# A hybrid encoder on one core: the block products' operand sums moved to the fifth and sixth tile of each feed-forward layer, and five pairs of tiles in block form instead of six

## The chip, the cores and the metric

The kernel runs on one core of one Trainium2 chip. The metric is device time in microseconds (us). Engines: TensorE (PE) multiplies, VectorE (DVE) and ScalarE (ACT) do the elementwise work, SyncE (SP) issues most DMAs.

## The reference

Two layers work on a sequence of 1040 columns (16 learned ones and 1024 inputs) of width 1024. Each layer adds a mixer and then a feed-forward part. The change lies in the feed-forward part alone:

```python
def swiglu(h, w_gate_up, w_down):
    gate, up = jnp.split(h @ w_gate_up.astype(h.dtype), 2, axis=-1)
    return (jax.nn.silu(gate) * up) @ w_down.astype(h.dtype)
```

`w_gate_up` is 1024 x 5632, so gate and up have 2816 rows each: 22 tiles of 128.

## The kernel before

All activations lie transposed, 128 features of a tile by the columns. A float32 product is made of three matmuls: each operand is split in a high part (ACT, a copy) and a low part (DVE, the rest), and high x high, high x low and low x high are added in PSUM. Weights are split as they arrive: `w_op` (line 1104 the high part on ACT, line 1105 the low part on DVE). `prod` (lines 1122, 1125, 1126) makes one product of four k-blocks, 12 matmuls.

The gate and up products run over tiles `f` = 0 to 21 (the first to the twenty-second), and a tile's two products are made in a form with seven products in place of eight (P1 to P7), the sums of weights S1 to S4 (lines 1464, 1465, 1473 or 1485, 1486) and sums of activations T1 to T4. The columns are two halves of 520 in the first layer and of 512 in the second (`l` = 1, where the first 16 columns are not needed). The first layer makes each product in two parts of 260 columns (`NJ` = 2), the second in one of 512. Products are evicted from PSUM by ACT (lines 1505, 1578) and DVE (1509, 1518 or 1566, 1569, 1573, 1582). `row_end` multiplies gate and up with the scale, applies silu, multiplies (lines 1438 to 1441) and stores the row to DRAM (1445); 1447 makes a difference for the later product.

**Block form.** The product P3 (S4 of the weights with B22 of the activations) of two neighbouring tiles is made together: the two S4 and the four quarters of B22 are taken as 2 x 2 blocks, and seven products of quarter size (6 matmuls each, 260 or 256 columns; `block`, lines 1530 to 1532) stand in place of eight. The even tile of a pair keeps its S4 in a tile `keep` (line 1485). The odd tile makes its own (line 1473) and four sums of the two (lines 1476 to 1479, tile `sm`), which are split by `w_op`. The activations' side needs sums of the quarters of B22, made once per layer: `block_operands` (lines 1422 to 1426 the sums in a scratch tile `t`, 1430 and 1431 their splits). Pairs are the tiles with `6 <= f < 18`, the seventh to the eighteenth.

**What sets the order.** Each engine works through its instructions in one fixed order. A scheduler makes it at build time from program order, priorities, dependences and buffers. A tile of a tag with `n` buffers waits until the tile before it in that buffer is read out. The tag "c" has two buffers, which `t`, `keep`, `sm` and the fourth tile's row (`early[3]`) share. Weights use two buffers of the tag "raw" and five of "ck2" (names raw and rw). `after(x, y)` makes `x` wait for `y`. `block_operands` is called behind the fifth tile (half of the sums: `TB[0]`, `TB[1]`) and behind the sixth (the other half, which needs a result of the first, `less`).

Of the kernel before, what the change touches and what calls it, by code (L numbers as in the profile page):

```python
# [11 lines left out]
ALU = mybir.AluOpType  # L12
# [30 lines left out]
def trunk(ctx: ExitStack, tc: tile.TileContext, xT, w_in, w_ba, w_out, w_gu, w_dn,  # L43
# [15 lines left out]
    def row(tag, dt=F32, bufs=1):  # L59
        return sb.tile([128, L], dt, tag=tag, bufs=bufs, name=nm(tag))  # L60
# [4 lines left out]
    def c4k(tag="c"):  # L65
        return sb.tile([128, L], F32, tag="c", bufs=2, name=nm(tag))
# [18 lines left out]
    def after(ins, prev):  # L85

        if prev is not None:
            tc.add_manual_dep(ins.ins, prev.ins.name, dep, reason="order")
        return ins
# [6 lines left out]
    tt = nc.vector.tensor_tensor  # L96
# [133 lines left out]
    def new_x(tags):  # L230
        (t0, t1, t2), r = tags
        A, B, C = big(t0, F32R), big(t1, F32R), big(t2, F32R)
        R = [row(r, F32R, 3) for _ in range(3)] + [row(r + "f", F32R)]
        return [(A[:, k, :], B[:, k, :]) for k in range(4)] + [(C[:, k, :], R[k]) for k in range(4)]


    x = new_x(S[0])
# [76 lines left out]
    for l in range(DEPTH):  # L314
# [24 lines left out]
        def trow():  # L339
            return row(Y[1], F32, 3)  # L340
# [360 lines left out]
        for pos, i in enumerate(seq):  # L701
# [4 lines left out]
            late = pos < (2, 1)[l]  # L706
            if pos < len(opened):
                t = opened[pos]
            else:
                t = trow()  # L710
# [72 lines left out]
        for i in range(4):  # L783
            t = trow()
# [3 lines left out]
            v = trow() if i % 2 == 0 else row(Y[1] + "f")  # L788
# [209 lines left out]
        for i in range(4):  # L998
            t = trow() if i < 2 else hb[1][:, i, :] if i < 3 else y3
# [28 lines left out]
        E = (L - o0) // 4  # L1028
# [105 lines left out]
        def part(t, z, j):  # L1134

            v = half(t[:, o0:L], z)
            return v[:, j, :] if NJ == 2 else v
# [10 lines left out]
        NE = 4  # L1148
# [33 lines left out]
        for m in range(KT + 2):  # L1182
# [11 lines left out]
            k = m - 2  # L1194
# [161 lines left out]
        def t_pair(t):  # L1356
            p, i = SEVEN[t // NP], t % NP
            hi, lo = t_slot(t)
            r = dw.pop(("b", t), None)
            held.pop(t, None)  # L1360
            if p in ("P5", "P6"):
                r = t_raw(i)
            elif p == "P7":
                behind(tt(out=r, in0=t_raw(i), in1=r, op=ALU.subtract))
            elif p == "P4":
                b21, r = r, t_raw(i)
                behind(tt(out=r, in0=b21, in1=r, op=ALU.subtract))
            act(out=hi, in_=r, func=AF.Copy)  # L1368
            behind(tt(out=lo, in0=r, in1=hi.bitcast(F32), op=ALU.subtract))
            if p == "P3":  # L1370
                tt(out=t_raw(i), in0=r, in1=t_raw(i), op=ALU.subtract)
# [14 lines left out]
        def down_begins(p):  # L1386
# [11 lines left out]
            elif p is p1_[2]:  # L1398
# [2 lines left out]
                w_unit(4)  # L1401
                t_load(3)
                t_pair(3)
        TB, us, rows, less = [], [], [], [None]

        def halves(t, n):
            return t[:, 0:n], t[:, n:2 * n]

        def quarter(k, j):
            return [t[:, k:k + 2, E * j:E * j + E] for t in T["B22"]]  # L1410

        def block_rows():
            rows.extend(row(Y[1], F32R, 3) for _ in range(3))
            rows.append(row(X[1], F32R, 3))
            us.extend(row(X[1], F32, 3) for _ in range(2))

        def block_operands(i):

            (b11, c11), (b12, c12), (b21, c21), (b22, c22) = ([t.bitcast(F32) for t in quarter(k, j)] for k in (0, 2) for j in (0, 1))
            x, cx, y, cy, p, q = (b22, c22, b12, c12, b21, c21) if i else (b12, c12, b11, c11, b22, c22)  # L1420
            va, vb = (t.rearrange("p (k e) -> p k e", k=2) for t in halves(c4k("t"), 2 * E))
            after(tt(out=va, in0=x, in1=y, op=ALU.subtract), row_before)
            tt(out=vb, in0=cx, in1=cy, op=ALU.subtract)
            tt(out=va, in0=va, in1=vb, op=ALU.add)
            tt(out=vb, in0=p, in1=less[0] if i else va, op=ALU.subtract)
            tt(out=vb, in0=vb, in1=q, op=ALU.add)
            less[0] = vb
            for r, v in zip(rows[i:i + 2], (va, vb)):
                h, w = (t.rearrange("p (k e) -> p k e", k=2) for t in halves(r, 2 * E))
                act(out=h, in_=v, func=AF.Copy)  # L1430
                tt(out=w, in0=v, in1=h.bitcast(F32), op=ALU.subtract)
                TB.append((h, w))

        def row_end(f, g, u, adds):

# [14 lines left out]
        row_before = None  # L1450
        first_of = None
        for f in range(FT):
            paired = 6 <= f < 18
            even, odd = paired and f % 2 == 0, paired and f % 2 == 1
            A11, A12, A21, A22 = raw4("raw"), raw4("raw"), raw4("ck2"), raw4("ck2")
            dma(A11, w_gu[l, f, 0, :, 0:4, :])
# [150 lines left out]
                row_end(f, g, u, adds)  # L1607
            if f == NE - 1:
                block_rows()
            if f in (NE, NE + 1):  # L1610
                block_operands(2 * (f - NE))


        hb = [big(X[0][0]), big(X[0][1])]
# [42 lines left out]
        for u, (p, b, m) in enumerate(UNITS):  # L1657
            if b == 1 and p in FIRST:
                dh, z = FIRST[p]
                q = 4 * dh + m  # L1660
# [13 lines left out]
            for j in range(NJ):  # L1674
# [10 lines left out]
                if b == NBK - 1:  # L1685
                    dh, z, op = TO[p]
                    h = part(hr[4 * dh + m], z, j)
                    read_out[u] = tt(out=h, in0=pin(ps), in1=h, op=op)

        if not last:  # L1690
            x = new_x(Y)
# [6 lines left out]
        else:  # L1698
# [22 lines left out]
            for (n0, n1) in FIN:  # L1721
                e = (n1 - n0) // 4
# [7 lines left out]
                for m in range(KT):  # L1730
                    h = hr[m][:, n0:n1]
# [93 lines left out]
```

## Time and profile before

| | us |
|---|---|
| timed runs, median of 3 | 2468.67 (2467.69 to 2473.94) |
| the profiled execution | 2466.03 |
| its span, first to last instruction | 2464.3 |
| PE busy in it | 2438.2 |
| DVE busy | 1834.9 |
| ACT busy | 1081.9 |

Times in the profile's rows are counted from the start of the span. A row of the timeline gives the start, the duration, the engine, the line, the output and inputs by name, the shape, and in brackets how long the engine had been idle and what ended that. In the table by stretches each engine has its busy time and its number of instructions, then come the granted clock of PE as a share (PEclk), the DMA engines' busy share and GB/s. A row of the waits reads: who waited for whom, us in total, times, longest. The gate and up products of the first layer run from 567.92 to 1020.77 us (first and last start), those of the second up to 2234.84.

### The profile page before, as it was taken

The page shows a single profiled execution, that of the slowest core. Times are in us where ns is not written, and L with a number is a line of the kernel's source. Part 1 is how long each engine was busy: PE and PEld are TensorE (multiplying, and loading weights), DVE is VectorE, ACT ScalarE, POOL GpSimd, SP SyncE. Part 2 cuts the span into 40 slices and gives each one's busy share as a digit, 9 for nine tenths or more (in the row PEclk, how much of TensorE's full clock was granted, in tenths as well). Part 3 has the DMA queues.
Part 4 walks back from the last instruction along what each step waited for, and adds up shares of the span by engine and source line. Part 5 has one row for each costly group of instructions (what it writes and reads, how often), then busy time and mean ns, then how long its engine had stood idle before and what let it go on. Part 6 is the DMA issues. An engine that isn't in the chain of part 4 may idle for free. (4 is left out here: it accounts for less than half of the span.)

```text
span 2464.3 us, 45203 instructions
## 1 busy us (share of the span) xinstructions
PE 2438.2 (99%) x17602; PEld 2256.7 (92%) x17602; DVE 1834.9 (74%) x3436; ACT 1081.9 (44%) x2028; POOL 66.3 (3%) x157
## 2 busy tenths in 40 slices
PE   9999999999999999999999999999999999999998
PEld 8999999999999999999999988998978788888887
DVE  6888346769888887977657984457797888778775
ACT  6654434536333333444445543345453333334544
POOL 0120000000000000000001100000000000000002
PEclk9999999999999999999999999999999999999999
DMA  4445345534222224674224453445332222337641
GB/s 134 160 156 185 118 134 158 182 101 134 100 78 104 84 86 137 223 243 143 92 81 155 155 179 111 152 144 194 121 124 98 82 94 99 119 130 251 198 136 69
DMA packets 201322, 335.27 MB, mean 136 GB/s; under 512 B 23404, under 2 KB 88356, under 8 KB 201108
## 3 DMA queue, kind: packets, MB, share of 16 engines
q1 hardware_dynamic: 172996, 293.83, 36.0%
q10 hardware_dynamic: 25936, 34.19, 4.3%
q0 software_dynamic: 2176, 4.36, 0.6%
q8 instruction: 138, 2.26, 0.4%
q14 instruction: 76, 0.62, 0.1%
HBM read 250.31 MB, written 81.99 MB: 135 GB/s over the span
## 5 line engine op out<-in xcount | busy, mean ns | idle before, releaser
L168 PE MATMUL pacc<-a,whi 128*128 128x346 f32 (+1 forms) x800 | 260.1, 326 | 0.7 <-ACT whi L138 0.4
L170 PE MATMUL pacc<-a,wlo 128*128 128x346 f32 (+1 forms) x800 | 259.0, 325 | 0.1
L168 PE MATMUL pacc<-b,whi 128*128 128x346 f32 (+2 forms) x672 | 232.4, 347 | 0.0
L170 PE MATMUL pacc<-b,wlo 128*128 128x346 f32 (+2 forms) x672 | 231.5, 346 | 0.0
L169 PE MATMUL pacc<-a,whi 128*128 128x346 f32 (+1 forms) x681 | 221.8, 326 | 0.2 <-DVE a L189 0.2
L138 ACT ACTIVATE whi<-raw 128x512 fp32r<-128x512 f32 x166 | 104.4, 631 | 236.8 <-PE pacc L169 195.1
L169 PE MATMUL pacc<-b,whi 128*128 128x346 f32 (+2 forms) x580 | 200.1, 345 | 0.0
L139 DVE TENSOR_TENSOR wlo<-raw,whi 128x512 fp32r<-128x512 f32 x166 | 114.0, 688 | 53.5 <-ACT whi L138 52.8
L168 PEld LDWEIGHTS pacc<-a,whi 128*128 128x128 f32 x800 | 150.5, 188 | 3.0 <-issue 1.0
L170 PEld LDWEIGHTS pacc<-a,wlo 128*128 128x128 f32 x800 | 150.7, 189 | 1.4 <-issue 0.8
L170 PEld LDWEIGHTS pacc<-b,wlo 128*128 128x128 f32 x672 | 126.4, 188 | 10.2 <-issue 1.7
L168 PEld LDWEIGHTS pacc<-b,whi 128*128 128x128 f32 x672 | 126.4, 188 | 9.8 <-issue 0.8
L169 PEld LDWEIGHTS pacc<-a,whi 128*128 128x128 f32 x681 | 128.3, 188 | 4.1 <-issue 2.1
L169 PEld LDWEIGHTS pacc<-b,whi 128*128 128x128 f32 x580 | 109.2, 188 | 7.9 <-issue 1.0
L1104 ACT ACTIVATE whi<-rw 128x512 fp32r<-128x512 f32 (+1 forms) x82 | 49.8, 615 | 107.4 <-PE pacc L1125 36.1
L1104 ACT ACTIVATE b<-rw 128x512 fp32r<-128x512 f32 (+1 forms) x63 | 38.7, 620 | 102.3 <-PE pacc L1125 29.0
L331 DVE TENSOR_TENSOR b<-pacc,rstd 128x346 f32<-128x346 f32 (+1 forms) x63 | 32.3, 513 | 49.0 <-PE pacc L170 46.3
L1104 ACT ACTIVATE a<-rw 128x512 fp32r<-128x512 f32 (+1 forms) x63 | 38.5, 618 | 64.4 <-PE pacc L1125 17.2
L331 DVE TENSOR_TENSOR a<-pacc,rstd 128x346 f32<-128x346 f32 (+2 forms) x59 | 32.6, 553 | 42.5 <-PE pacc L170 41.9
L1105 DVE TENSOR_TENSOR wlo<-rw,whi 128x512 fp32r<-128x512 f32 (+1 forms) x82 | 54.1, 666 | 9.9 <-ACT whi L1104 9.4
L1368 ACT ACTIVATE P<-a 128x512 fp32r<-128x512 f32 x63 | 38.3, 625 | 25.4 <-PE pb L1684 19.7
L1368 ACT ACTIVATE P<-b 128x520 fp32r<-128x520 f32 x63 | 37.2, 628 | 27.1 <-PE pacc L1684 20.1
(1129 smaller groups left out, 8019.0 us busy)
## 6 DMA issues: line engine op xcount, KB each, us to landing
raw<-in_w_in SPq DMA_DIRECT2D x110, 256.0 KB
raw<-in_w_gu SPq DMA_DIRECT2D x104, 256.0 KB
rw<-in_w_gu SPq DMA_DIRECT2D x88, 256.0 KB
rw<-in_w_dn SPq DMA_DIRECT2D x90, 192.0 KB
rec<-vkd SPq DMA_DIRECT2D x61, 256.0 KB
raw<-in_w_out SPq DMA_DIRECT2D x48, 256.0 KB
b<-ad SPq DMA_DIRECT2D x45, 260.0 KB
a<-ad SPq DMA_DIRECT2D x45, 256.0 KB
```

The costliest lines, as they stand in the source:

```text
L138: whi_done[0] = hasten(wpr, lambda: act(out=hi, in_=raw[:, 0:kk, :], func=AF.Copy))
L139: whi_done[1] = hasten(wpr, lambda: tt(out=lo, in0=raw[:, 0:kk, :], in1=hi.bitcast(F32), op=ALU.subtract))
L168: mm(ps[:, :n], wh, xh[:, n0:n1], start=(i == 0), stop=False)
L169: mm(ps[:, :n], wh, xl[:, n0:n1], start=False, stop=False)
L170: last_mm[0] = mm(ps[:, :n], wl, xh[:, n0:n1], start=False, stop=(i == K - 1))
L331: tt(out=t[:, n0:n1], in0=ps, in1=rstd[:, n0:n1], op=ALU.mult)
L1104: hasten(wpr, lambda: act(out=hi, in_=src, func=AF.Copy))
L1105: hasten(wpr, lambda: tt(out=lo, in0=src, in1=hi.bitcast(F32), op=ALU.subtract))
L1368: act(out=hi, in_=r, func=AF.Copy)
```

## The change

The tiles in block form are now those with `8 <= f < 18`, so the seventh and eighth tile get P3 of their own. `block_operands` is called twice behind the sixth tile: the first call makes the operands 0, 1 and 3 (7 sums), the second operand 2 (3 sums). The second sum of each call waits for the fifth tile's row (`gate`); the first (`cx` less `cy`) waits for nothing but its buffer. The number of sums (10) and splits (4) per layer stays.

```diff
-        TB, us, rows, less = [], [], [], [None]
+        TB, us, rows, gate = {}, [], [], []
...
-        def block_operands(i):
+        def block_operands(late):
 
             (b11, c11), (b12, c12), (b21, c21), (b22, c22) = ([t.bitcast(F32) for t in quarter(k, j)] for k in (0, 2) for j in (0, 1))
-            x, cx, y, cy, p, q = (b22, c22, b12, c12, b21, c21) if i else (b12, c12, b11, c11, b22, c22)
             va, vb = (t.rearrange("p (k e) -> p k e", k=2) for t in halves(c4k("t"), 2 * E))
-            after(tt(out=va, in0=x, in1=y, op=ALU.subtract), row_before)
-            tt(out=vb, in0=cx, in1=cy, op=ALU.subtract)
-            tt(out=va, in0=va, in1=vb, op=ALU.add)
-            tt(out=vb, in0=p, in1=less[0] if i else va, op=ALU.subtract)
-            tt(out=vb, in0=vb, in1=q, op=ALU.add)
-            less[0] = vb
-            for r, v in zip(rows[i:i + 2], (va, vb)):
-                h, w = (t.rearrange("p (k e) -> p k e", k=2) for t in halves(r, 2 * E))
+            x, cx, y, cy = (b22, c22, b12, c12) if late else (b12, c12, b11, c11)
+
+            def put(n, v):
+                h, w = (t.rearrange("p (k e) -> p k e", k=2) for t in halves(rows[n], 2 * E))
                 act(out=h, in_=v, func=AF.Copy)
                 tt(out=w, in0=v, in1=h.bitcast(F32), op=ALU.subtract)
-                TB.append((h, w))
+                TB[n] = h, w
+
+            tt(out=vb, in0=cx, in1=cy, op=ALU.subtract)
+            after(tt(out=va, in0=x, in1=y, op=ALU.subtract), gate[0])
+            tt(out=va, in0=va, in1=vb, op=ALU.add)
+            put(2 if late else 0, va)
+            for n, p, q, less in () if late else ((1, b22, c22, va), (3, b21, c21, vb)):
+                tt(out=vb, in0=p, in1=less, op=ALU.subtract)
+                tt(out=vb, in0=vb, in1=q, op=ALU.add)
+                put(n, vb)
...
-            paired = 6 <= f < 18
+            paired = 8 <= f < 18
...
-            if f in (NE, NE + 1):
-                block_operands(2 * (f - NE))
+            if f == NE:
+                gate.append(row_before)
+            if f == NE + 1:
+                block_operands(False)
+                block_operands(True)
```

Lines below the change have new numbers: 1430 and 1431 (the splits) are now 1425 and 1426; the sums are 1429 (the first), 1430, 1431, 1434 and 1435; what stood at 1438 to 1587 stands four lines lower (1105 and 1122 to 1126 don't move).

The order moves at these places. **First, DVE in the second layer, in the sixth tile's work.** Behind an eviction (old line 1573, new 1577) stood one sum and the splits of weights:

```order
L1573 TENSOR_TENSOR b_2079_20446<-pb_20630,b_2079_20446 128x2x256
L1426 TENSOR_TENSOR t_20583<-t_20583,a_1985_19834 128x512
L1105 TENSOR_TENSOR b_2027_20050<-raw_20740,b_2027_20050 128x512
L1473 TENSOR_TENSOR rw_20864<-raw_20857,rw_20865 128x512
L1105 TENSOR_TENSOR b_2027_20050<-rw_20858,b_2027_20050 128x512
L1431 TENSOR_TENSOR a_2075_20442<-t_20583,a_2075_20442 128x512
```

and now stand more of the sums, up to the next eviction (line 1570):

```order
L1577 TENSOR_TENSOR b_2074_20434<-pb_20608,b_2074_20434 128x2x256
L1105 TENSOR_TENSOR b_2022_20038<-rw_20729,b_2022_20038 128x512
L1426 TENSOR_TENSOR a_2070_20430<-t_20707,a_2070_20430 128x512
L1469 TENSOR_TENSOR rw_20872<-rw_20871,raw_20863 128x512
L1426 TENSOR_TENSOR a_2071_20431<-t_20721,a_2071_20431 128x512
L1434 TENSOR_TENSOR t_20707<-a_1980_19822,t_20707 128x512
L1105 TENSOR_TENSOR b_2022_20038<-rw_20872,b_2022_20038 128x512
L1435 TENSOR_TENSOR t_20707<-t_20707,a_1980_19822 128x512
L1570 TENSOR_TENSOR b3f_20761<-pacc_20763,b_2073_20433 128x2x256
```

Four of the sums' instructions stand between these two evictions now.

**Second, DVE in the second layer, at the kept S4 of the first pair.** Before, in the seventh tile's work, the second call's sums stood ahead of it, and the sm sums right behind it:

```order
L1422 TENSOR_TENSOR t_20729<-a_1985_19834 128x512
L1424 TENSOR_TENSOR t_20729<-t_20729 128x512
L1425 TENSOR_TENSOR t_20729<-a_1985_19834,t_20583 128x512
L1582 TENSOR_TENSOR b_2078_20445<-pf_20777,b_2078_20445 128x512
L1431 TENSOR_TENSOR a_2076_20443<-t_20729,a_2076_20443 128x512
L1426 TENSOR_TENSOR t_20729<-t_20729,a_1985_19834 128x512
L1485 TENSOR_TENSOR keep_20757<-raw_20740,rw_20748 128x512
L1509 TENSOR_TENSOR b_2079_20446<-pb_20895,b_2079_20446 128x2x256
L1439 TENSOR_TENSOR b_2078_20445<-b_2078_20445,rstd_19168 128x1024
L1431 TENSOR_TENSOR b_2077_20444<-t_20729,b_2077_20444 128x512
L1105 TENSOR_TENSOR b_2027_20050<-keep_20757,b_2027_20050 128x512
L1476 TENSOR_TENSOR sm_20875<-rw_20864 128x256
```

Now, in the ninth tile's work, no sum of the activations stands there:

```order
L1451 TENSOR_TENSOR a3f_20605<-b_2074_20434 128x512
L1105 TENSOR_TENSOR wlo_21014<-rw_21007,whi_21013 128x512
L1469 TENSOR_TENSOR rw_21008<-rw_21007,raw_20999 128x512
L1513 TENSOR_TENSOR b_2074_20434<-pb_20899,b_2074_20434 128x2x256
L1489 TENSOR_TENSOR keep_21017<-raw_21000,rw_21008 128x512
L1105 TENSOR_TENSOR b_2022_20038<-rw_21008,b_2022_20038 128x512
L1105 TENSOR_TENSOR b_2022_20038<-raw_21116,b_2022_20038 128x512
```

The kept S4 now comes 20 DVE instructions ahead of the first sm sum; it came five ahead.

**Third, DVE in the first layer, at the split of the sm sums of the first pair.** Before, the next tile's first weight sum (line 1464) stood ahead of it:

```order
L1479 TENSOR_TENSOR sm_7931<-keep_7732,sm_7931 128x256
L1582 TENSOR_TENSOR a_753_7232<-pacc_7833,a_753_7232 128x260
L1464 TENSOR_TENSOR rw_8194<-rw_8188,rw_8189 128x512
L1105 TENSOR_TENSOR a_690_6565<-sm_7931,a_690_6565 128x512
L1439 TENSOR_TENSOR a_753_7232<-a_753_7232,rstd_5575 128x1040
L1509 TENSOR_TENSOR a_754_7233<-pa_7967,a_754_7233 128x260
```

and now it stands behind both splits (lines 1105 of sm) and the eviction at line 1513:

```order
L1483 TENSOR_TENSOR sm_8391<-keep_8192,sm_8391 128x256
L1105 TENSOR_TENSOR a_690_6565<-sm_8391,a_690_6565 128x512
L1577 TENSOR_TENSOR a_753_7232<-pb_8293,a_753_7232 128x260
L1105 TENSOR_TENSOR wlo_8399<-sm_8391,whi_8398 128x512
L1105 TENSOR_TENSOR a_690_6565<-rw_8374,a_690_6565 128x512
L1513 TENSOR_TENSOR a_754_7233<-pacc_8411,a_754_7233 128x260
L1468 TENSOR_TENSOR rw_8654<-rw_8648,rw_8649 128x512
```

The weight sum, which waits for a DMA, went from ahead of both splits of sm to behind them.

## Prediction

> **What bounds the kernel now.** I read the page first: which engine is full, and which one the chain that ended last runs through.
>
> ```profile
> span 2464.3 us, 45203 instructions
> PE 2438.2 (99%) x17602; PEld 2256.7 (92%) x17602; DVE 1834.9 (74%) x3436; ACT 1081.9 (44%) x2028; POOL 66.3 (3%) x157
> PE 42%; DVE 2%; DMA 1%; ACT 0%; issue 0%; SPq 0%; DVEq 0%
> ```
>
> PE is busy for 99% of the span, so the time is what PE has to stream, plus the places where it stands still or streams slowly. An edit on DVE or ACT counts only where PE waits for it. So the second view is who PE waited for, over the whole run, longest first. These are its first four rows and one further down.
>
> ```profile
> PE pf L1530 <- ACT b L1104: 3.2, 1, 3.2
> PE pf L1532 <- DVE b L1105: 1.8, 1, 1.8
> PE pa L1122 <- ACT b L1104: 1.4, 1, 1.4
> PE pa L765 <- ACT b L777: 1.2, 1, 1.2
> PE pacc L1532 <- DVE a L1105: 1.1, 1, 1.1
> ```
>
> Lines 1530 to 1532 are the small matmuls of the block products. All their waits stand in one pair of tiles per layer, the first one (seventh and eighth tile). The busy time of each engine in the stretches behind it, which hold the other pairs and the tiles after them, shows that:
>
> ```profile
> 730.00:1000.00 270.00, 270.00 (x2253) 270.00 (x2253) 221.91 (x389) 97.89 (x185) 0.00 (x0) 1.00 0.31 104
> 1948.00:2180.00 232.00, 232.00 (x1117) 193.17 (x1116) 185.03 (x291) 85.90 (x142) 0.00 (x0) 1.00 0.30 102
> ```
>
> PE is busy for 270.00 of 270 us and for 232.00 of 232, at clock 1.00: no pair but the first makes PE wait. Now PE's instructions in order of time, at the first pair of the first layer and then of the second:
>
> ```profile
> 722.06 0.28 PE L1125 MATMUL pacc<-P,whi 128*128 128x260 f32 x1
> 723.49 0.39 PE L1532 MATMUL pacc<-b,a 128*128 128x260 f32 x1 [1.15 <-DVE a L1105]
> 723.95 0.28 PE L1532 MATMUL pacc<-b,a 128*128 128x260 f32 x1
> 724.98 0.39 PE L1530 MATMUL pa<-b,a 128*128 128x260 f32 x1 [0.74 <-DVE a L1509]
> ...
> 729.22 0.29 PE L1126 MATMUL pf<-P,wlo 128*128 128x260 f32 x1
> ```
>
> ```profile
> 1935.35 0.40 PE L1126 MATMUL pf<-b,wlo 128*128 128x512 f32 x1
> 1938.99 0.39 PE L1530 MATMUL pf<-a,b 128*128 128x256 f32 x1 [3.25 <-ACT b L1104]
> ...
> 1941.27 0.58 PE L1532 MATMUL pf<-a,b 128*128 128x256 f32 x1 [1.77 <-DVE b L1105]
> ...
> 1947.77 0.28 PE L1530 MATMUL pf<-a,b 128*128 128x256 f32 x1
> 1947.89 0.28 PE L1531 MATMUL pf<-a,b 128*128 128x256 f32 x1
> ```
>
> The bracketed idle time is not the whole loss. Matmuls start back to back at these distances (252 of 260 columns in 30 us; 132, nearly all of 512 columns, in 30 us), and more slowly behind the waits, where the granted clock (PEclk, the third number from the end) is halved:
>
> ```profile
> 690.00:720.00 30.00, 30.00 (x252) 30.00 (x252) 27.04 (x50) 10.84 (x22) 0.00 (x0) 1.00 0.27 89
> 725.50:729.20 3.70, 3.67 (x18) 3.41 (x18) 3.70 (x9) 1.81 (x4) 0.00 (x0) 0.54 0.20 68
> 1900.00:1930.00 30.00, 30.00 (x132) 24.30 (x131) 20.55 (x31) 8.16 (x13) 0.00 (x0) 1.00 0.19 70
> 1941.00:1947.70 6.70, 5.73 (x21) 4.95 (x22) 6.70 (x15) 3.32 (x6) 0.00 (x0) 0.50 0.09 22
> ```
>
> So one matmul of 260 columns takes 30/252 = 0.119 us, one of 512 columns 30/132 = 0.23, one of 256 columns 0.12 (1947.77 to 1947.89). First layer: from 722.06 to 729.22 stand 25 matmuls, 2.98 us of work in 7.16: **4.2 us lost**. Second layer: from 1935.35 to 1947.77 stand 21 of 256 columns and 3 of 512, 2.5 + 0.7 = 3.2 us of work in 12.42: **9.2 us lost**. Together 13.4 us.
>
> The Trainium skill, "TensorE: Matmul & The Clock Gate", section "What's actually happening", says that the clock halves after at least one idle window of about 3.4 us. The first layer's waits are 1.15 and 0.74 us, and the clock was at half behind them all the same, so the trace disagrees. By that rule the first layer would have lost only its two gaps, 2.3 us instead of 4.2, and the sum below would come out 1.9 us higher.
>
> **Why PE waits there.** DVE's order at the seventh tile of the second layer, in its rows and the ACT row between them:
>
> ```profile
> 1928.81 0.69 DVE L1582 TENSOR_TENSOR b<-pb,b 128x512 f32<-128x512 f32 x1 [5.17 <-PE pb L1126]
> ...
> 1933.35 0.68 DVE L1422 TENSOR_TENSOR t<-a 128x512 f32<-128x512 f32 x1
> ...
> 1937.59 0.69 DVE L1485 TENSOR_TENSOR keep<-raw,rw 128x512 f32<-128x512 f32 x1
> ```
>
> ```profile
> 1938.31 0.63 ACT L1104 ACTIVATE b<-keep 128x512 fp32r<-128x512 f32 x1
> ```
>
> The kept S4 (keep, line 1485) takes a buffer of the "c" tag, which has two. Both are held by the sums' scratch tiles until line 1425 of the second call has read the first one, so keep comes after it, in DVE's queue behind four of the second call's five sums. ACT splits keep at 1938.31, and PE, which was through with the work before at about 1935.6, starts at 1938.99. The splits of sm and of the sums follow in the same queue, hence the later waits. In the first layer the same queue was held once more, by a weight load that had not landed:
>
> ```profile
> 722.14 0.69 DVE L1464 TENSOR_TENSOR rw<-rw,rw 128x512 f32<-128x512 f32 x1 [1.36 <-DMA rw<-in_w_gu]
> 722.75 0.69 DVE L1105 TENSOR_TENSOR a<-sm,a 128x512 fp32r<-128x512 f32 x1
> ```
>
> Line 1105 at 722.75 is what PE's line 1532 waited for at 723.49.
>
> **The change, part by part.** *Both waits go.* All sums now stand in the sixth tile's work, and the first kept S4 belongs to the ninth tile. In the order shown with the change, it then stands well ahead of the first sm sum, with no scratch tile between. The first pair is then built like the second pair was before, which waited for nothing. In the first layer the split of sm stands ahead of the next tile's line 1464 (1468 now), so a late load no longer holds it. I take all of the loss: -13.4 us; it could be nothing if the wait only moves.
>
> *Two tiles less in block form.* Per layer, two P3 products come back and one block goes. First layer: 2 x 2 x 12 = 48 matmuls of 260 columns for 42 of 260: +6 x 0.119 = +0.7 us. Second: 24 x 0.23 for 42 x 0.12: 5.5 - 5.0 = +0.5 us. All of it lies on PE, so on the path: **+1.2 us**. The DVE sums and splits of that block go too (20 DVE instructions fewer in the whole program), which is worth nothing where PE doesn't wait.
>
> *The sums move up.* There are 14 DVE instructions per layer (ten sums and four splits), of about 0.6 us each from start to start (722.14 to 722.75 above): 8.4 us. Half of them stood there before, so the sixth tile's DVE work grows by 4.2 us. In the second layer the idle time of 5.17 us ahead of 1928.81, just behind this work, hides it. In the first, 30 us hold 27.04 of DVE work (690 to 720, which takes in both old calls). What is queued behind a sum are evictions and weight splits. By the order (the first place shown with the change), the longest run without an eviction in it is seven instructions, four of the sums' and three of the weights', between lines 1577 and 1570 of the second layer: 4.2 us. Between the ends of the two products that these lines evict stand 20 matmuls of 0.23 on PE, 4.6 us, so the second eviction is hardly late. I take 0; the upper bound is a wait like the one of 1.15 us, with the half clock behind it, in both layers: 2 x 4.2 us.
>
> *A new wait.* The first sum has lost its gate and stands in the fifth tile's work. Its scratch tile reuses the buffer that the fourth tile's row is stored from, so it waits for that store, and DVE's queue behind it waits too. The store's issue, and the longest such wait on a store that I find:
>
> ```profile
> 669.50 0.33 SPq L1445 DMA_DIRECT2D ad<-c  x1
> 935.59 0.38 SPq L1445 DMA_DIRECT2D ad<-a  x1
> ```
>
> ```profile
> 941.17 0.39 ACT L1505 ACTIVATE a<-pb 128x260 f32<-128x260 f32 x1 [5.16 <-DMA ad<-a]
> 672.55 0.42 DVE L1582 TENSOR_TENSOR a<-pb,a 128x260 f32<-128x260 f32 x1
> 677.59 0.28 PE L1122 MATMUL pb<-P,a 128*128 128x260 f32 x1
> ```
>
> That store took 5.6 us from issue to release, so this one would be through by 675.1. DVE reaches the sum at about 672.9, behind line 1582 at 672.55. It is held for 2.2 us at worst, and then needs 0.6 for the sum and 0.7 for the two evictions (lines 1566 and 1569) that PE's product at 677.59 waits for: 676.4, 1.2 us to spare. I take 0, at worst a wait as above.
>
> **The sum.** -13.4 + 1.2 = -12.2 us. The profiled execution took 2466.03 us (span 2464.3), which gives 2453.8; the median of the three timed runs is 2468.67, 2.6 above it, and I forecast in its terms: **2456.5 us**.
>
> **Rivals.** *The wait moves along.* The chain of keep, sm, splits, then block products is the same in the new first pair; were it the chain itself that is too long and not the sums in its way, 13.4 us come back and 1.2 stay: 2469.9. Against it: the pairs behind the first, built the same way, kept PE busy for 270.00 of 270 us. *Part of it comes back*: a late weight load (1.36 us at 722.14) or the sums hold an eviction in one layer or both, at the first layer's price of 4.2 us with the half clock: 2460.7 or 2464.9. For it: DVE has 27 us of work in 30 there. Against it: the idle 5.17 us in the second layer. *Slower*: all 14 instructions end up ahead of evictions that PE needs in the sixth tile. Then PE stands for 8.4 us per layer and streams 6.7 us at half clock as behind 1941, +3.4: 2 x 11.8 + 1.2 - 13.4 = +11.4, so 2480. It gives a slower kernel only from 13.4 - 1.2 = 12.2 us of new losses on, 6.1 per layer. Against it: scheduled evictions stand between the sums, not behind them all. That the change doesn't do what it says is ruled out by the order of the built program.
>
> **How the numbers follow.** Both waits go: 0.74, 2452 to 2460.5 (1.9 us by which the first layer's loss hangs on the half clock, and the spread of the timed runs). Part comes back: 0.13, 2460 to 2466. The wait moves along: 0.07, 2468 to 2472. Slower: 0.06. A measurement tells about 0.3% from no change, 7.4 us: faster below 2461.3. That is the first case and about half of the second: 0.80. Within: the rest of the second and the third, 0.14. Slower: 0.06. The range from 2452 to 2466 takes in the first two cases and leaves 0.13 out.
>
> **What would show it.** Right: no wait of lines 1534 to 1536 (the block's matmuls by their new numbers) in PE's waits, PEclk at 1.00 in all stretches of both layers' gate and up products, and PE busy all the time there. The first step is wrong if PE waits at the ninth and tenth tile for a split of keep or sm; the cover of the moved sums is gone if PE waits in the fifth to seventh tile for lines 1570, 1573, 1577 or 1513. The +1.2 us shows as 12 matmuls fewer in the program, six more in the first layer and 18 fewer, but wider, in the second. A bank or a weight slot whose turn shifts in the later tiles and brings a wait there would make the prediction wrong in a way that I haven't priced.

## The result and the profile after

The changed kernel takes **2461.93 us** (median of six timed runs, 2457.09 to 2462.56), the kernel before 2468.99 beside it (six runs, 2467.69 to 2473.94). The ratio is 0.9962, with an interval of 0.9949 to 0.9975. The medians differ by 7.1 us; the ratio means 9.4 us less, 6.2 to 12.6. The forecast was 2456.5, 12.2 us less. The profiled execution of the changed kernel took 2462.14 us.

These are the lines of its page that answer to those shown of before.

```profile
span 2460.3 us, 45143 instructions
PE 2437.2 (99%) x17590; PEld 2254.5 (92%) x17590; DVE 1830.4 (74%) x3416; ACT 1079.3 (44%) x2020; POOL 66.8 (3%) x157
PE 41%; DVE 2%; DMA 1%; ACT 0%; issue 0%; DVEq 0%; SPq 0%; ACTq 0%
```

PE has 12 matmuls fewer and DVE 20 instructions fewer, as counted in the prediction. The span is 3.9 us shorter than in the profile of before (2464.25 and 2460.33). Who PE waits for in the second layer's gate, up and down stages (1790 to 2400 us), all of it:

```profile
PE pa L1122 <- ACT b L1104: 1.4, 1, 1.4
PE pacc L1688 <- DVE b L1695: 0.8, 1, 0.8
PE pacc L1691 <- DVE a L1321: 0.7, 1, 0.7
```

No wait at the block's matmuls (lines 1534 to 1536) is left. The first row is that of before; the other two are new and stand in the down product. The busy times of the engines in the stretches of both layers that hold the moved sums and all pairs:

```profile
640.00:700.00 60.00, 60.00 (x503) 60.00 (x502) 51.22 (x89) 20.98 (x35) 0.00 (x0) 1.00 0.31 102
700.00:760.00 60.00, 60.00 (x502) 60.00 (x501) 50.27 (x88) 21.65 (x40) 0.00 (x0) 1.00 0.27 89
760.00:1020.00 260.00, 260.00 (x2170) 260.00 (x2170) 215.21 (x377) 100.25 (x188) 0.00 (x0) 1.00 0.34 111
1900.00:1960.00 60.00, 60.00 (x261) 48.61 (x260) 52.02 (x79) 20.76 (x34) 0.00 (x0) 1.00 0.29 97
1960.00:2180.00 220.00, 220.00 (x1054) 182.98 (x1053) 173.62 (x271) 79.95 (x132) 0.00 (x0) 1.00 0.30 98
```

PE is busy for the whole of each at clock 1.00, so the stage that was changed does what was forecast. The rest has to be sought elsewhere. For that I cut every profile of this case at PE's rows: the first gate or up matmul (line 1122) of each layer, and the last high x high matmul of its down product (line 1681 in the kernel before, 1688 in the changed one), all at their starts. The stretches (us) of all eleven profiles, those of the experiments below included:

| profile | ahead of the first gate product | first layer's gate, up, down | between | second layer's gate, up, down | tail | half-clock stretches begin at |
|---|---|---|---|---|---|---|
| before | 567.92 | 632.64 | 587.37 | 615.99 | 60.33 | 725.8, 1940.9 (double) |
| before again | 568.40 | 630.97 | 588.21 | 617.66 | 60.10 | 1939.1 (triple) |
| changed | 573.83 | 629.24 | 587.89 | 609.58 | 59.78 | 10.8, 58.5 |
| changed again | 569.83 | 629.23 | 588.93 | 611.72 | 60.66 | 55.3, 205.5, 2253.5 |
| sums alone | 570.94 | 628.48 | 588.20 | 613.34 | 60.16 | 207.6, 1835.7 |
| pairs alone | 568.11 | 629.24 | 588.44 | 609.96 | 59.78 | none |
| bank turn | 570.33 | 629.31 | 587.91 | 609.82 | 59.82 | 55.6 |
| slot turn | 570.50 | 629.24 | 588.09 | 607.91 | 59.85 | 55.9 |
| one scratch | 569.81 | 630.67 | 586.14 | 618.25 | 59.80 | 56.5, 1937.3 (triple) |
| early gate | 568.42 | 628.51 | 589.11 | 609.84 | 59.80 | none |
| six pairs, gated | 568.02 | 628.07 | 587.99 | 614.39 | 59.78 | 1937.0 (double) |

(A half-clock stretch is 3.41 us long, a double one 6.83, a triple one 10.24. Each profile has one more, left out of the table: it begins at 2448.7 to 2459.5 and runs past the end of the span.) From before to the changed kernel the first layer gives 3.4 us and the second 6.4, and 5.9 us go back in the part **ahead of the first changed instruction**, where the two programs are the same. Two stretches at half clock are in that part. At 1.7 us each they make 3.4 of the 5.9 us. The rest is small waits: by PE's rows 1.4 us between 90 and 130 us and 0.5 us up to 490, without half clock, and the little that is left near the two stretches. Three windows of the changed kernel's profile:

```profile
10.80:14.10 3.30, 3.13 (x11) 3.14 (x12) 2.79 (x6) 3.13 (x7) 0.00 (x0) 0.50 1.06 385
14.10:58.50 44.40, 43.61 (x336) 37.70 (x335) 29.96 (x47) 23.41 (x36) 0.00 (x0) 1.00 0.27 84
58.60:61.90 3.30, 3.30 (x19) 2.61 (x17) 2.32 (x7) 3.27 (x5) 0.00 (x0) 0.50 0.49 158
```

PE is busy in the first and the last (3.13 and 3.30 us of 3.30), but at PEclk 0.50. So three questions were open: why the pair no longer waits, where the two new waits in the down product come from, and whether the 5.9 us belong to the change at all.

### The profile page after: what moved, and what is told of

It reads as the page before. It is cut to its first block, busy times and chain, and to the rows that moved or that the text cites. A ratio compares the mean times of both kernels' runs of the same rounds, so it can differ in the third digit from the quotient of the medians.

```text
span 2460.3 us, 45143 instructions
## 1 busy us (share of the span) xinstructions
PE 2437.2 (99%) x17590; PEld 2254.5 (92%) x17590; DVE 1830.4 (74%) x3416; ACT 1079.3 (44%) x2020; POOL 66.8 (3%) x157
## 5 line engine op out<-in xcount | busy, mean ns | idle before, releaser
L170 PEld LDWEIGHTS pacc<-b,wlo 128*128 128x128 f32 x672 | 126.4, 188 | 10.3 <-issue 1.7
L1104 ACT ACTIVATE b<-rw 128x512 fp32r<-128x512 f32 x64 | 39.5, 624 | 105.9 <-PE pacc L1125 30.2
```

The lines of the kernel that those rows point to most:

```text
L170: last_mm[0] = mm(ps[:, :n], wl, xh[:, n0:n1], start=False, stop=(i == K - 1))
L1104: hasten(wpr, lambda: act(out=hi, in_=src, func=AF.Copy))
```

## Experiments

The pairs alone and the two runs marked (kernel before) are edits of the kernel before; the other edits start from the changed kernel. All have five or more timed runs, beside the kernel before, whose median lay between 2468.4 and 2469.5 us.

### The sums alone (six pairs)

```diff
-            paired = 8 <= f < 18
+            paired = 6 <= f < 18
```

> The sums in their new place, but six pairs as before (twelve tiles). In the built program the kept S4 of the first pair then stands 12 instructions earlier in DVE's queue than before, and the split of sm stands ahead of the next tile's first weight sum. Theory 1 (the place of the sums made PE wait): both waits at the first pair go all the same, and no P3 products come back, so 13.4 us off the kernel before, some 1 us better than the changed kernel: ratio 0.9945 to 0.9960. Rival (the room of one more pair of tiles is what took the wait away): PE waits at the seventh and eighth tile as before, 6 to 13 us of it stay, ratio 0.998 to 1.000.

Measured: 2459.99 us, ratio 0.9967 (0.9955 to 0.9980). The first layer comes out as theory 1 has it, 628.48 us against 632.64: all of the 4.2 us is gone with the pair where it was. The second layer's stages take 613.34, only 2.6 us less than before. Its two largest waits besides the old one:

```profile
PE pa L1122 <- DVE a L1573: 2.2, 1, 2.2
...
PE pf L1534 <- ACT sm L1542: 1.0, 1, 1.0
```

The second stands at the first pair: about 1 us of its wait is left. The first is a new one near 1832 us, some 100 us ahead of the first pair. DVE's rows there, in the kernel with the sums alone:

```profile
1830.36 0.69 DVE L1468 TENSOR_TENSOR rw<-rw,rw 128x512 f32<-128x512 f32 x1 [1.95 <-DMA rw<-in_w_gu]
1830.97 0.69 DVE L1105 TENSOR_TENSOR wlo<-rw,whi 128x512 fp32r<-128x512 f32 x1
1831.57 0.69 DVE L1570 TENSOR_TENSOR a<-pb,b 128x512 f32<-128x512 f32 x1
...
1833.97 0.69 DVE L1573 TENSOR_TENSOR a<-pa,a 128x512 f32<-128x512 f32 x1
```

and of the changed kernel, at the same place:

```profile
1831.70 0.68 DVE L1570 TENSOR_TENSOR a<-pb,b 128x512 f32<-128x512 f32 x1
1833.62 0.69 DVE L1468 TENSOR_TENSOR rw<-rw,rw 128x512 f32<-128x512 f32 x1 [1.23 <-DMA rw<-in_w_gu]
1834.23 0.68 DVE L1105 TENSOR_TENSOR wlo<-rw,whi 128x512 fp32r<-128x512 f32 x1
1834.83 0.68 DVE L1573 TENSOR_TENSOR a<-pa,a 128x512 f32<-128x512 f32 x1
```

The scheduler has put one eviction (line 1570) behind a weight sum (line 1468) whose load lands late, and line 1573, for which PE waits, three instructions further back. So the place of the sums takes the wait away where the tiles are the same; the rival falls for the first layer. In the second, the other order at 1832 costs 2.4 us and a half-clock stretch behind it, so the ratio missed what theory 1 said.

### The pairs alone (sums in two calls, as before)

```diff
-            paired = 6 <= f < 18
+            paired = 8 <= f < 18
```

> Ten tiles in block form, but the sums in their old place, in two calls behind the fifth and the sixth tile. Theory 1 (the sums stand ahead of the first kept S4 and hold it): the kept S4 now belongs to the ninth tile, one pair later than the sums, so the waits go without the sums being moved: 12 us off, ratio 0.9945 to 0.9965, as the changed kernel. Rival (the sums' place is what matters): the second call's sums still hold the evictions or the weight splits, PE waits 3 us or more in the seventh to tenth tile, ratio 0.998 to 1.000.

Measured: 2459.54 us, ratio 0.9963 (0.9951 to 0.9976). Both layers' stages are those of the changed kernel within 0.4 us (629.24 and 609.96), and its new waits in the down product are there too. Each half of the change takes the first pair's wait away by itself (the sums alone all but 1 us of it in the second layer), so the two halves don't add up.

### The turn of the banks

```diff
+            if f == 7:
+                bn[0] += 1 if NJ == 2 else 2
```

> The changed kernel, with the counter of the PSUM banks moved on by the one (first layer) or two (second layer) banks that the omitted block would have taken, behind the eighth tile. The banks of all later products then have the turn that they had before. Theory 2 (the 0.83 and 0.73 us that PE newly waits at 2253 to 2255, in the second layer's down product, come from the shifted turn of the banks): they go, 2.0 us less than the changed kernel, and the down stage has the length of before, about 616 us less 8.7 for the second layer's gate, up and down products together. Rival (they come from another order of the weight splits on DVE, whatever the banks): they stay, and the time is that of the changed kernel within 1 us.

Measured: 2459.86 us, ratio 0.9967 (0.9955 to 0.9979), and PE's waits in the down product are still there, now at 2249 to 2251 us:

```profile
PE pb L1690 <- DVE b L1697: 0.8, 1, 0.8
PE pacc L1693 <- DVE a L1321: 0.7, 1, 0.7
```

The bank in which the first of them appears has changed (pb for pacc); their size hasn't, and the stages take 609.82 us for the changed kernel's 609.58. Theory 2 falls.

### The changed kernel once more

> The changed kernel once more, nothing altered. Its timed runs lay at 2462 and at 2457, and in its profiled execution the part ahead of the first changed instruction was 5.9 us longer than in that of the kernel before, with two stretches of 3.4 us at half clock, at 10 and at 58 us. Theory 3 (that part varies from run to run, and hides part of the gain): this profile may show none, one or two of those stretches; the prologue is then 568 to 574 us, and the span follows it one to one, with the gate, up and down stages alike within 0.5 us. Rival (the changed kernel has a longer prologue, from its code or its data's place in memory): the prologue is 573 us or more again, with both stretches.

Measured: 2460.36 us (2458.5 to 2462.14), ratio 0.9967 (0.9955 to 0.9980). The prologue takes 569.83 us, 4.0 less than in the first profile of the very same program, so the rival falls. The expectation missed in one thing: the later stages were not alike within 0.5 us. This execution had a half-clock stretch right behind the waits in the down product (1.7 us), its old wait at line 1122 was 1.9 us instead of 1.4, and the second layer took 2.1 us more. The busy times there, with PEclk at 0.50:

```profile
2253.60:2256.90 3.30, 3.30 (x9) 2.56 (x8) 3.30 (x8) 0.53 (x1) 0.00 (x0) 0.50 0.89 303
```

### The turn of the weight slots

What else does an omitted pair shift? Weights are split into seven slots in turn (`wn`, line 1088); a pair takes 16 of them, two plain tiles 14.

```diff
+            if f == 7:
+                wn[0] += 2
```

> The changed kernel, with the counter of the seven weight slots moved on by two behind the eighth tile, as the omitted pair would have moved it (a pair takes 16 slots, two plain tiles 14). In the built program the second layer's down product then begins 56 matmuls ahead of the last gate and up product, as in the kernel before, and not 89 as in the changed one. Theory 2b (the shifted turn of the weight slots reorders the end of the second layer's gate and up stage, and so brings the waits of 0.83 and 0.73 us at 2253 to 2255): they go, the second layer's gate, up and down stages take 607.0 to 608.5 us together instead of 609.6, ratio about 0.9955, some 2 us better than the changed kernel. Rival (that end of the layer is full on DVE in any order): a wait of the same size stands there or near by, and the stages take 609 us or more.

Measured: **2457.36 us** (2456.34 to 2458.0), ratio 0.9955 (0.9942 to 0.9967). All of PE's waits in the second layer's gate, up and down stages:

```profile
PE pa L1122 <- ACT b L1104: 1.4, 1, 1.4
```

Both waits are gone, and the stages take 607.91 us. By PE's rows the down product begins 12.9 us ahead of the last gate or up matmul, as before, and 20.5 us ahead of it in the changed kernel. What the other order did there is seen in the changed kernel. First PE, then DVE:

```profile
2252.42 0.40 PE L1690 MATMUL pb<-P,whi 128*128 128x512 f32 x1
2253.65 0.47 PE L1688 MATMUL pacc<-P,a 128*128 128x512 f32 x1 [0.83 <-DVE b L1695]
2253.96 0.40 PE L1690 MATMUL pacc<-P,a 128*128 128x512 f32 x1
2255.09 0.51 PE L1691 MATMUL pacc<-P,a 128*128 128x512 f32 x1 [0.73 <-DVE a L1321]
```

```profile
2252.36 0.55 DVE L1317 TENSOR_TENSOR rw<-rw,a 128x384 f32<-128x384 f32 x1
2252.82 0.68 DVE L1695 TENSOR_TENSOR b<-pacc,b 128x512 f32<-128x512 f32 x1
2253.43 0.68 DVE L1369 TENSOR_TENSOR P<-a,P 128x512 fp32r<-128x512 f32 x1
2254.03 0.55 DVE L1317 TENSOR_TENSOR rw<-rw,a 128x384 f32<-128x384 f32 x1
2254.49 0.55 DVE L1321 TENSOR_TENSOR a<-rw,a 128x384 fp32r<-128x384 f32 x1
```

DVE has no idle time. PE waits first for a bank that line 1695 evicts, then for the split of a down weight (line 1321). Between matmuls 0.23 apart stand gaps of 1.23 and 1.13 us: 1.0 + 0.9 lost. (Between the two kernels' stages the difference is 1.7 us.) By their intervals the timed runs alone would not tell this kernel from the changed one (0.9942 to 0.9967 and 0.9955 to 0.9980); the stage does, since the four profiles with ten tiles and the shifted slots have 609.6 to 611.7 us there.

### One scratch tile for both calls (kernel before)

This tests the cause that the prediction gave, the buffer of tag "c".

```diff
-            va, vb = (... for t in halves(c4k("t"), 2 * E))
+            if not i:
+                less[0] = c4k("t")
+            va, vb = (... for t in halves(less[0], 2 * E))
...
+            if i:
+                after(tt(out=vb, in0=p, in1=vb, op=ALU.subtract), row_before)
+                tt(out=vb, in0=vb, in1=q, op=ALU.add)
+                put(3, vb)
```

> The kernel before with its six pairs, and the sums in two calls in their old places; only the second call uses the first one's scratch tile again, and forms its sum from the first call's remainder before it writes over it (the same instructions in another order). So the kept S4 of the first pair takes the other buffer of its tag, which has long been free. In the built program it then stands ahead of all of the second call's sums but the first, some 37 instructions earlier; the sums of sm still stand behind them. Theory 1 (the buffer that the scratch held made PE wait in the second layer): the wait of 3.25 us for the split of the kept S4 goes, and most of the 9.2 us lost there, 5 to 8 us; in the first layer, where PE waited for the split of sm, about the 4.2 us stay. Ratio 0.997 to 0.998. Rival (the mass of the sums on DVE is what makes PE wait, whatever the buffer): the kept S4 comes early, but the split of sm or an eviction is late by as much, and less than 2 us are gained, ratio 0.999 to 1.0.

Measured: 2467.03 us, ratio 1.0 (0.9991 to 1.0009). **Theory 1 falls.** The kept S4 does come early, at 1909.99 us instead of 1937.59. But PE now waits once, for 7.74 us, where it had waited for 3.25 and 1.77 us and twice more for less than 0.5. The sums' gate and the sm row in DVE's rows of the kernel before:

```profile
1931.28 1.22 DVE L1441 TENSOR_TENSOR b<-b,a3f 128x1024 f32<-128x1024 f32 x1
...
1941.80 0.42 DVE L1477 TENSOR_TENSOR sm<-sm,keep 128x256 f32<-128x256 f32 x1
```

In this run, DVE's rows, then ACT's and PE's:

```profile
1909.99 0.68 DVE L1495 TENSOR_TENSOR keep<-raw,rw 128x512 f32<-128x512 f32 x1
...
1930.41 1.22 DVE L1451 TENSOR_TENSOR b<-b,a3f 128x1024 f32<-128x1024 f32 x1
...
1932.48 0.68 DVE L1432 TENSOR_TENSOR t<-a,t 128x512 f32<-128x512 f32 x1
...
1941.68 0.42 DVE L1487 TENSOR_TENSOR sm<-sm,keep 128x256 f32<-128x256 f32 x1
```

```profile
1942.13 0.63 ACT L1104 ACTIVATE b<-sm 128x512 fp32r<-128x512 f32 x1 [1.89 <-DVE sm L1487]
```

```profile
1942.81 0.58 PE L1540 MATMUL pb<-a,b 128*128 128x256 f32 x1 [7.74 <-ACT b L1104]
```

Line 1451 (1441 in the kernel before) is the last product of the sixth tile's row, on which the second call's first sum is made to wait. All five of its sums stand behind it here, and the sums of sm behind them: the third row of sm begins at 1941.68, and in the kernel before at 1941.80. (Counted from the layer's first gate product that is 155.1 and 153.9 us.) The buffer decided which of the two splits PE waits for, not when the pair is ready. The second layer's stages take 618.25 us, 2.3 more than in the first profile of before, with three half-clock stretches for two. The first layer's take 630.67, as in the second profile of before (630.97): its loss has moved to other waits, the longest 0.6 us at line 1122.

### The second call's gate one row earlier (kernel before)

```diff
-            after(tt(out=va, in0=x, in1=y, op=ALU.subtract), row_before)
+            after(tt(out=va, in0=x, in1=y, op=ALU.subtract), gate[0])
...
+            if f == NE:
+                gate.append(row_before)
```

> The kernel before with its six pairs and its two calls of the sums; only the second call's first sum is made to follow the fifth tile's row, as the first call's, and no longer the sixth tile's. In the built program nine of the ten sums and their splits then stand in the sixth tile's work. Theory 1c (what made PE wait is the second call's gate: its sums can't begin before the sixth tile's row is done, and the sums of sm come behind them): the waits at the first pair go in both layers, at most 1 us of the 9.2 stays in the second. But the order at the start of the second layer's gate and up stage is that of the run with the sums alone, an eviction (line 1566) behind a weight sum whose load comes late (line 1464): so PE waits about 2.2 us near 1832 again, with 1.7 us at half clock if the grid falls so. Ratio 0.996 to 0.997; the first layer's gate, up and down stages take about 628.5 us together, the second's 611 to 614. Rival (the mass of the sums is what counts, wherever they are gated): evictions wait in the sixth tile instead, the first pair's loss comes back there, ratio 0.999 to 1.0.

Measured: **2457.45 us** (2454.16 to 2459.0), ratio 0.9950 (0.9937 to 0.9962). The sums, the keep and sm of the second layer in DVE's rows, and the first pair in the busy times:

```profile
1911.35 1.29 DVE L1422 TENSOR_TENSOR t<-a 128x512 f32<-128x512 f32 x2
...
1926.91 0.69 DVE L1485 TENSOR_TENSOR keep<-raw,rw 128x512 f32<-128x512 f32 x1
...
1929.10 0.42 DVE L1477 TENSOR_TENSOR sm<-sm,keep 128x256 f32<-128x256 f32 x1
```

```profile
690.00:760.00 70.00, 70.00 (x587) 70.00 (x587) 63.33 (x115) 27.54 (x52) 0.00 (x0) 1.00 0.29 97
1905.00:1935.00 30.00, 30.00 (x133) 24.42 (x132) 28.18 (x45) 11.84 (x20) 0.00 (x0) 1.00 0.20 70
1935.00:1945.00 10.00, 10.00 (x54) 8.43 (x53) 9.97 (x16) 3.30 (x7) 0.00 (x0) 1.00 0.39 135
```

The third row of sm begins 12.7 us earlier than in the kernel before (10.8 counted from the layer's first gate product), and PE waits at no pair in either layer. The stages take 628.51 and 609.84 us, the second less than the 611 to 614 that were expected, and so the ratio lies below the range given. One edge moved from the sixth tile's row to the fifth's does what the whole change does, with six pairs. The forecast wait near 1832 is there too (2.2 us, at line 1122 for line 1569), this time with no half-clock stretch behind it. In the first layer the split of sm now stands ahead of the weight sum of line 1464 (718.49 and 719.09 us) that held it before, so there no run separates the gate from the late load.

### Six pairs, all first sums gated

```diff
-            tt(out=vb, in0=cx, in1=cy, op=ALU.subtract)
+            after(tt(out=vb, in0=cx, in1=cy, op=ALU.subtract), gate[0])
```

> The sums in their new place and six pairs, as in the run with the sums alone, but the first difference of each half follows the fifth tile's row as well, so that no sum stands early in the second layer. In the built program the eviction of line 1570 at the start of that layer's gate and up stage then stands ahead of the weight sum of line 1468 whose load comes late, as in the kernel before and in the changed one. Theory 1c and the order of that place: the wait of 2.2 us near 1832 goes with its half clock, and of the first pair's loss 0 to 1.2 us stay in the second layer: the stages take 628.5 us in the first layer and 607 to 609 us in the second, ratio 0.9945 to 0.9955, as good as the changed kernel with the slots' turn put right, or 1 us better. Rival (the sums' place in the sixth tile is too full with all of them gated): evictions of the sixth tile or the splits for the seventh are late in the first layer, where DVE has 27 us of work in 30, 2 us or more, ratio 0.9965 or more.

Measured: 2460.5 us, ratio 0.9966 (0.9952 to 0.9979). Half of this was right: the wait near 1832 is gone, as the order said, and the first layer has the best time of all (628.07). But the second layer's first pair waits again, in PE's waits:

```profile
PE pb L1536 <- DVE b L1105: 2.2, 1, 2.2
...
PE pf L1534 <- ACT sm L1542: 1.0, 1, 1.0
```

Behind it come 6.83 us at half clock (1937.0), and the stages take 614.39 us. The ratio is the rival's, but the place isn't: PE waits in the second layer, not in the first. With all ten sums behind the gate the split of sm comes 2 us too late there. That the amount of work behind the gate counts as well as the gate is read from this order and not tested by itself.

### The kernel before once more

> The kernel before once more. Theory 3 (stretches of 3.41 us at half clock, on a grid of 3.41 us whose phase differs from execution to execution, come and go in the unchanged parts, at about 10, 55 and 206 us, and cost 1.7 us each): the prologue is 568 to 574 us by how many of them this execution has, and the two gate and up stages take 632 to 633 and 614 to 616 us with the down stages, as they did. Its first pair waits as before (1.15 us in the first layer, 3.25 us in the second); how many half-clock stretches follow them may differ by one. Rival (the kernel before has a shorter prologue than the changed one for some reason in the program): 568 us again, without a half-clock stretch ahead of 600 us.

Measured: 2467.93 us, ratio 0.9999 (0.9990 to 1.0007). The prologue took 568.40 us with no half-clock stretch, which is what the rival said and theory 3 allowed; this run alone settles nothing there. The other profiles do: without a stretch ahead of 565 us the prologue takes 567.9 to 568.4 (five profiles, three of them of changed programs), with one 569.8 to 570.9 (four), with two 569.8 and 573.8. The first pair's loss was cut otherwise than in the first profile. In the first layer the same wait, 0.79 us long instead of 1.15 (PE's row),

```profile
723.74 0.39 PE L1532 MATMUL pacc<-b,a 128*128 128x260 f32 x1 [0.79 <-DVE a L1105]
```

was followed by no half clock (the busy times right behind it, PEclk at 1.00),

```profile
726.00:732.00 6.00, 5.92 (x49) 5.71 (x49) 5.71 (x13) 2.57 (x6) 0.00 (x0) 1.00 0.37 112
```

and in the second layer the half clock lasted three stretches instead of two (the same view there):

```profile
1939.20:1949.20 10.00, 7.58 (x28) 6.47 (x28) 8.93 (x18) 4.22 (x8) 0.00 (x0) 0.50 0.27 84
```

So the stages took 1.7 us less in the first layer and 1.7 us more in the second, both outside the ranges that were expected (632 to 633 and 614 to 616).

## Why the prediction came out as it did

- **Both waits go, -13.4 us**: right. With the +0.7 us for the P3 products, the first layer was to give 3.5 us and gave 3.4. The second was to give 8.7; it gives 6.4, and 8.1 with the slots' turn put right. That the two layers' share was 4.2 and 9.2 us hung on that one execution: in the other profile of before it would be 2.5 and 10.9, with the same sum.
- **The cause**, the buffer held by the first scratch tile: wrong. With the buffer free the pair was ready at the same time (1941.68 for 1941.80), and nothing was gained. The second call's gate on the sixth tile's row is what made PE wait in the second layer: moved alone, it takes the wait away. In the first layer moving it takes the wait away too, together with the order behind a late weight load that the prediction named; which of the two counts there stays open. The prediction read the keep's wait in DVE's queue rightly, but didn't follow what stands ahead of it back to the edge that holds it all. That the change worked all the same is in part luck: it moves the sums and the first pair, and either alone is enough.
- **+1.2 us for two tiles less in block form**: of the right size. The first layer takes 629.24 us with five pairs and 628.51 with six and the early gate, 0.7 apart. No run isolates the second layer's 0.5.
- **The moved sums cost nothing, the new wait on the fourth tile's store costs nothing**: right. PE is busy for all of 640 to 760 us, and the sum that takes the stored buffer, forecast for 672.9 us (678.8 with the longer prologue), has no idle time ahead of it:

```profile
678.80 0.69 DVE L1429 TENSOR_TENSOR t<-b 128x520 f32<-128x520 f32 x1
```

- **The step of the sum that failed** is the last one named, "a bank or a weight slot whose turn shifts in the later tiles", which the sum priced at nothing. It was the weight slot: 1.9 us in the second layer's down product (1.7 by the stages), and 1.7 more where a half-clock stretch follows.
- **The base**: the prediction added 2.6 us to go from the profiled execution to the median. That difference has the size of one or two half-clock stretches (half of 3.41 us each), and six of the eleven profiles have such stretches in the prologue, that one none; this is argued from sizes, not shown. The changed kernel's executions differ in the same way: its profile with two stretches took 2462.14 us, and its timed runs at 2457.1 have a mean clock of 0.998 and 0.999, those at 2462 one of 0.997. With -12.2 + 1.9 = -10.3 us the kernel would stand within the interval of the ratio (6.2 to 12.6 us less); the forecast of -12.2 stands within it too, so the timed runs alone don't show the miss, the stages do. Not all of the spread is half clock: the part between the layers, which has no half-clock stretch in any profile, differs by 0.8 and 1.0 us between two executions of the same program. What of the rest is half clock and what is the measurement's own spread stays open.
- **Faster or not**: the prediction counted as faster what lies below 2461.3 us. The median is 0.6 us above that; the ratio's interval, 0.9949 to 0.9975, lies below 1 as a whole.
- **The rivals**: that the wait moves along, and that it comes back in part, didn't happen in the changed kernel. Both happened in experiments, with one scratch tile (all of it in the second layer) and with all sums gated (3.6 us of waits and the half clock).

## What to carry to other kernels

When an instruction is late in a queue, follow back what stands ahead of it until an edge or a load holds all of it; here, freeing a buffer in between only changed who was waited for. When work is dropped from a rotation (slots, banks), everything later gets another turn, and a scheduler may choose another order: put the counter where it would have been, and compare. Below 0.3%, compare stages of several profiles, not totals: here unchanged code differed by 5.9 us between the two kernels' profiles, and by 4.0 between two of the same kernel.

## What the runs showed of the hardware

The half-clock stretches lie on a grid. All but each profile's last one, which the end cuts off, are 3.41 us long or a whole multiple of it, and within one execution they begin whole multiples of 3.413 us apart: 47.8 us in the changed kernel (14 steps), 150.2 and 2048.0 in its second profile (44 and 600), 1215.1 in the kernel before (356). From execution to execution the grid lies differently, so the same wait is followed by none, one or several stretches of half clock, at 1.7 us each where PE streams. The Trainium skill, "TensorE: Matmul & The Clock Gate", section "What's actually happening", describes such a window of 3413 ns that runs free, with a phase that differs from run to run; these traces agree. What the Trainium skill states there for the return to half clock, at least one idle window, they don't bear out. By PE's rows, PE stood idle for 1.87 of 3.41 us in the window ahead of the stretch at 725.8 in the kernel before, and for 0.54 us ahead of the one at 55.9 in the kernel with the slots' turn put right, while 1.47 us near 1829 in the kernel with the early gate (its grid is that of its last stretch) were followed by none. What exactly is counted in the window, these runs don't tell.
